# A row softmax with temperature on one core: eight-row tiles under a scheduler against sixteen-row tiles in four-row blocks under a written-out order

## The chip, the cores and the metric

The kernel runs on one core of one Trainium2 chip. The metric is the device time of one execution in microseconds (us), taken as the median of several runs. One further number comes from a profiled execution: its span, from its first to its last instruction, which the views of the profile divide up.

## What is computed

The input has 16 x 1024 rows of 512 float32 values, and each row is put through a softmax after division by 0.5:

```python
x_scaled = x / temp                                   # temp = 0.5
x_max = np.max(x_scaled, axis=-1, keepdims=True)
exp_x = np.exp(x_scaled - x_max)
return exp_x / np.sum(exp_x, axis=-1, keepdims=True)
```

The 16,384 rows come to 33.55 MB, which are read once and written once. A row fits in one partition, so no data passes between partitions.

## The kernel before

The rows are cut into 16 tiles of 128 partitions x G = 8 rows (L26). In the main memory the eight rows of a partition stand one behind the other, so a partition's share of a tile is one run of 16 KB and a tile is 2 MB. The tiles live in a pool of eight buffers (L35), and all work is done in place.

For each tile the loop at L42 issues, in this order:

- the load of the tile on the queue of SyncE (SP), L44;
- one VectorE reduction over all eight rows, giving the negative maximum of each, L47;
- eight ScalarE activations, one a row, exp(2x - max) with the sum of the row as a second output, L51. Subtracting the maximum of x itself, not of 2x, changes numerator and denominator alike;
- the reciprocal of the eight sums on VectorE, L61;
- on VectorE one multiplication of rows 2 to 7 by their reciprocals, the reciprocals being read as a second tensor that is broadcast along the row, L65;
- on ScalarE the scaling of rows 0 and 1, a copy with a per-partition factor, L71;
- the store of the whole tile on the queue of GpSimd (POOL), L78.

Nothing in the kernel fixes how the tiles follow one another on an engine: the tile framework orders the instructions by its own estimate and puts in the waits. A load has to wait for the store of the tile that had its buffer before, eight tiles earlier. The first eight loads wait for nothing.

Of the kernel before, what the change touches and what calls it, by code (L numbers as in the profile page):

```python
# [1 line left out]

# [4 lines left out]


@with_exitstack  # L10
def kernel(
    ctx: ExitStack,
    tc: tile.TileContext,
    x: bass.AP,
    out: bass.AP,
):
    nc = tc.nc
    fp32 = mybir.dt.float32
    P = nc.NUM_PARTITIONS

    D = x.shape[-1]
    xf = x.flatten_outer_dims()
    of = out.flatten_outer_dims()
    N = xf.shape[0]

    G = 8  # L26
    C = N // (P * G)
    assert C * P * G == N

    N_ACT_NORM = 2  # L30

    xr = xf.rearrange("(c p g) d -> c p g d", p=P, g=G)
    outr = of.rearrange("(c p g) d -> c p g d", p=P, g=G)

    data = ctx.enter_context(tc.tile_pool(name="data", bufs=8))  # L35
    stats = ctx.enter_context(tc.tile_pool(name="stats", bufs=8))

    AX = mybir.AxisListType.X
    EXP = mybir.ActivationFunctionType.Exp
    COPY = mybir.ActivationFunctionType.Copy  # L40

    for c in range(C):  # L42
        xt = data.tile([P, G, D], fp32, name="xt")
        nc.sync.dma_start(out=xt, in_=xr[c])  # L44

        negmax = stats.tile([P, G], fp32, name="negmax")
        nc.vector.reduce_max(negmax, xt, axis=AX, negate=True)  # L47

        sums = stats.tile([P, G], fp32, name="sums")
        for g in range(G):  # L50
            nc.scalar.activation(  # L51
                out=xt[:, g, :],
                in_=xt[:, g, :],
                func=EXP,
                bias=negmax[:, g : g + 1],
                scale=2.0,
                accum_out=sums[:, g : g + 1],
            )

        recip = stats.tile([P, G], fp32, name="recip")  # L60
        nc.vector.reciprocal(recip, sums)  # L61

        if N_ACT_NORM < G:
            k = N_ACT_NORM
            nc.vector.tensor_mul(  # L65
                xt[:, k:, :],
                xt[:, k:, :],
                recip[:, k:].unsqueeze(2).broadcast_to((P, G - k, D)),
            )
        for g in range(N_ACT_NORM):  # L70
            nc.scalar.activation(  # L71
                out=xt[:, g, :],
                in_=xt[:, g, :],
                func=COPY,
                scale=recip[:, g : g + 1],
            )

        nc.gpsimd.dma_start(out=outr[c], in_=xt)  # L78


# [1 line left out]
_INS = ['x']  # L82
_OUTS = [((16, 1024, 512), 'float32')]


# [23 lines left out]
```

The softmax here doesn't subtract the row's maximum and nothing guards it: scores larger than these inputs give would overflow.

## Time and profile before

| what | value |
|---|---|
| median of 5 runs | 164.64 us (163.82 to 164.75) |
| the profiled execution's own time | 163.82 us |
| its span | 161.7 us |
| VectorE busy | 124.5 us (77% of the span), 48 instructions |
| ScalarE busy | 112.5 us (70%), 289 instructions |
| GpSimd busy | 8.8 us (5%) |
| moved by DMA | 67.13 MB, mean 415 GB/s over the span |

The profiled execution took 163.82 us, of which 161.7 are its span; the remaining 2.1 us lie around it. It was the quickest of the five runs, 0.82 us under the median, and this distance has to be kept in mind when a sum made on the span is set against the median.

How to read the views: the page begins with busy time by engine; then the span is cut into 40 slices, with a digit for the busy tenth of each engine in a slice, and the mean busy share of the 16 DMA engines below it. After that come the DMA queues (q1 is SyncE's, "hardware_dynamic"; q0 is GpSimd's, "software_dynamic"), the chain of work that ended last, and groups of instructions by line with the mean duration of one in ns. A busy engine is only a bound if the others wait for it in the end.

### The profile page before, as it was taken

Reading aid. Unit: us, or ns where it says so; the run is one execution under the profiler, and the core shown is the slowest. Engines: PE = TensorE matmul, PEld = TensorE weight load, DVE = VectorE, ACT = ScalarE, POOL = GpSimd, SP = SyncE. Lnnn points to the kernel's source line nnn. Section 1 sums busy time; section 2 is a strip of 40 time slices with the busy share of each in tenths; the row PEclk is TensorE's granted clock in tenths of the full one; section 3 lists DMA queues with packets and bytes.
Section 4 is the critical chain, followed back from the end, with each engine's and each line's share of the span. In section 5 each row is a group of like instructions: output and inputs, shape, how many; then the busy total and the mean of one; then the engine's idle time right before and its main releaser. Section 6 shows DMA issues by size and latency. Waiting matters only on the chain.

```text
span 161.7 us, 483 instructions
## 1 busy us (share of the span) xinstructions
DVE 124.5 (77%) x48; ACT 112.5 (70%) x289; POOL 8.8 (5%) x20
## 2 busy tenths in 40 slices
DVE  0088799999999999695986959689595986999100
ACT  0037997999999998949397593957939397595000
POOL 0000010010101010101001010100101001011100
DMA  5999999999999999999999999999999999999993
GB/s 146 438 434 418 446 430 381 422 444 426 426 446 422 426 446 418 434 442 418 438 428 430 434 430 426 442 426 430 438 426 434 438 422 430 442 418 434 413 442 134
DMA packets 4610, 67.13 MB, mean 415 GB/s; under 512 B 512, under 2 KB 512, under 8 KB 512
## 3 DMA queue, kind: packets, MB, share of 16 engines
q1 hardware_dynamic: 2304, 33.56, 49.3%
q0 software_dynamic: 2304, 33.56, 48.6%
q14 instruction: 2, 0.02, 0.0%
HBM read 33.55 MB, written 33.55 MB: 415 GB/s over the span
## 4 chain that ended last, share of the span: by engine, by line
DMA 61%; DVE 18%; ACT 8%; issue 7%; POOLq 0%; SPq 0%
DMA xt<-in_x_dram 37%; DMA out_dram<-xt 23%; DVE negmax L47 11%; ACT xt L51 7%; DVE xt L65 6%; ACT xt L71 1%; DVE recip L61 0%; POOLq L104 0%; SPq L44 0%; POOLq L78 0%
## 5 line engine op out<-in xcount | busy, mean ns | idle before, releaser
L51 ACT ACTIVATE xt<-xt,negmax 128x512 f32<-128x512 f32 x128 | 90.5, 710 | 26.4 <-DVE negmax L47 26.4
L47 DVE TENSOR_REDUCE negmax<-xt 128x8 f32<-128x4096 f32 x16 | 70.4, 4403 | 24.2 <-DMA xt<-in_x_dram 24.2
L65 DVE TENSOR_TENSOR xt<-xt,recip 128x3072 f32<-128x3072 f32 x16 | 53.6, 3350 | 0.1
L51 ACT ACTIVATION_READ_ACCUMULATOR xt<-xt,negmax 128x1 f32 x128 | 24.2, 189 | 0.0
L71 ACT ACTIVATE xt<-xt,recip 128x512 f32<-128x512 f32 x32 | 21.1, 709 | 0.3 <-DVE recip L61 0.3
L78 POOL DMA_DIRECT2D out_dram<-xt x16 | 8.6, 540 | 142.0 <-ACT xt L51 87.4
L51 ACT ACT_TABLE_LOAD x1 | 1.3, 1283 | 8.8 <-DMA xt<-in_x_dram 8.8
L61 DVE RECIPROCAL recip<-sums 128x8 f32<-128x8 f32 x16 | 3.1, 196 | 1.2 <-ACT xt L51 1.2
L93 POOL MEMSET const-float32-0.0<- 128x1 f32 x1 | 0.1, 98 | 0.2 <-issue 0.2
L93 POOL MEMSET const-bfloat16-1.0<- 128x1 bf16 x1 | 0.1, 101 | 0.0
L93 POOL MEMSET const-float32-1.0<- 128x1 f32 x1 | 0.1, 98 | 0.0
L93 POOL MEMSET const-uint8-127<- 128x1 uint8 x1 | 0.1, 98 | 0.0
## 6 DMA issues: line engine op xcount, KB each, us to landing
xt<-in_x_dram SPq DMA_DIRECT2D x16, 2048.0 KB, 26.8
out_dram<-xt POOLq DMA_DIRECT2D x16, 2048.0 KB, 17.9
```

The lines of the kernel that those rows point to most:

```text
L47: nc.vector.reduce_max(negmax, xt, axis=AX, negate=True)
L51: nc.scalar.activation(out=xt[:, g, :], in_=xt[:, g, :], func=EXP, bias=negmax[:, g : g + 1], scale=2.0, accum_out=sums[:, g : g + 1],)
L61: nc.vector.reciprocal(recip, sums)
L65: nc.vector.tensor_mul(xt[:, k:, :], xt[:, k:, :], recip[:, k:].unsqueeze(2).broadcast_to((P, G - k, D)),)
L71: nc.scalar.activation(out=xt[:, g, :], in_=xt[:, g, :], func=COPY, scale=recip[:, g : g + 1],)
L78: nc.gpsimd.dma_start(out=outr[c], in_=xt)
L93: nc = _bacc.Bacc("TRN2", target_bir_lowering=False, num_devices=1)
```

## The change

The tile grows to G = 16 rows (one run of 32 KB a partition, 4 MB a tile, eight tiles), in six buffers. The order on every engine is now the order of the program text (`manual_schedule`). Work goes in blocks of B = 4 rows, 32 in all, and the loop over blocks puts later steps of earlier blocks behind the first steps of the current one: in step i, VectorE gets the maximum of block i and then the scaling of block i - 1; ScalarE gets the exponentials of block i, then the scaling of its one row of block i - 2, then, where block i - 3 was the last of its tile, the store of the whole tile.

The scaling on VectorE becomes three instructions a block, each one row times a per-partition factor. ScalarE scales one row in four, as before. The maximum is multiplied by 2 in a small extra instruction, so 2 max is what is subtracted. Stores leave GpSimd's queue and go to ScalarE's. The first tile is loaded in two pieces: rows 0 to 3 through ScalarE's queue, rows 4 to 15 through SyncE's. A one-element exponential at the start brings the load of the activation table forward.

The core of the diff (function bodies that keep their operation are cut):

```diff
-    G = 8
+    G = 16
+    B = 4
+    N_ACT = 1
-    data = ctx.enter_context(tc.tile_pool(name="data", bufs=8))
-    stats = ctx.enter_context(tc.tile_pool(name="stats", bufs=8))
+    FIRST = [(0, 4), (4, 16)]
+    data = ctx.enter_context(tc.tile_pool(name="data", bufs=6))
+    stats = ctx.enter_context(tc.tile_pool(name="stats", bufs=6))
+    ctx.enter_context(tc.manual_schedule())
-        nc.sync.dma_start(out=xt, in_=xr[c])
+        for lo, hi in FIRST if c == 0 else [(0, G)]:
+            queue = nc.scalar if (c, lo) == (0, 0) else nc.sync
+            queue.dma_start(out=xt[:, lo:hi, :], in_=xr[c][:, lo:hi, :])
-        nc.vector.reduce_max(negmax, xt, axis=AX, negate=True)
+        nc.vector.tensor_reduce(negmax, xb, axis=AX, op=MAX, negate=True)
+        nc.vector.tensor_scalar_mul(bias, negmax, 2.0)
-            nc.vector.tensor_mul(
-                xt[:, k:, :],
-                xt[:, k:, :],
-                recip[:, k:].unsqueeze(2).broadcast_to((P, G - k, D)),
-            )
+        for g in range(B - N_ACT):
+            nc.vector.tensor_scalar_mul(xb[:, g, :], xb[:, g, :], recip[:, g : g + 1])
-        nc.gpsimd.dma_start(out=outr[c], in_=xt)
+    def store(i):
+        c, b = blocks[i]
+        if b + B == G:
+            nc.scalar.dma_start(out=outr[c], in_=tiles[c])
+    load(0)
+    warm = stats.tile([P, 1], fp32, name="warm", bufs=1)
+    nc.vector.memset(warm, 0.0)
+    nc.scalar.activation(out=warm, in_=warm, func=EXP)
+    n = len(blocks)
+    for i in range(n + 3):
+        if i < n:
+            if blocks[i][1] == 0 and i:
+                load(blocks[i][0])
+            shift(i)
+            exponentials(i)
+        if 1 <= i <= n:
+            scale_vector(i - 1)
+        if 2 <= i <= n + 1:
+            scale_scalar(i - 2)
+        if 3 <= i:
+            store(i - 3)
```

`shift` holds the reduction and the doubling, `exponentials` the four exponentials, `scale_vector` the reciprocal and the three products, `scale_scalar` ScalarE's row.

More of the change, by code (lines that the diff above doesn't have):

```diff
@@ L19 @@
     P = nc.NUM_PARTITIONS
+    AX = mybir.AxisListType.X
+    EXP = mybir.ActivationFunctionType.Exp
+    COPY = mybir.ActivationFunctionType.Copy
+    MAX = mybir.AluOpType.max
     D = x.shape[-1]
@@ L24, with load, shift, exponentials @@
     N = xf.shape[0]
-    G = 8
+    G = 16
+    B = 4
+    N_ACT = 1
     C = N // (P * G)
     assert C * P * G == N
-    N_ACT_NORM = 2
     xr = xf.rearrange("(c p g) d -> c p g d", p=P, g=G)
     outr = of.rearrange("(c p g) d -> c p g d", p=P, g=G)
-    data = ctx.enter_context(tc.tile_pool(name="data", bufs=8))
-    stats = ctx.enter_context(tc.tile_pool(name="stats", bufs=8))
[L38 to L43, printed above, removed]
-        nc.sync.dma_start(out=xt, in_=xr[c])
[L46 to L50, printed above, removed]
+    FIRST = [(0, 4), (4, 16)]
+    data = ctx.enter_context(tc.tile_pool(name="data", bufs=6))
+    stats = ctx.enter_context(tc.tile_pool(name="stats", bufs=6))
+    ctx.enter_context(tc.manual_schedule())
+    tiles = {}
+    blocks = [(c, b) for c in range(C) for b in range(0, G, B)]
+    state = {}
+    def load(c):
+        xt = tiles[c] = data.tile([P, G, D], fp32, name="xt")
+        for lo, hi in FIRST if c == 0 else [(0, G)]:
+            queue = nc.scalar if (c, lo) == (0, 0) else nc.sync
+            queue.dma_start(out=xt[:, lo:hi, :], in_=xr[c][:, lo:hi, :])
+    def shift(i):
+        c, b = blocks[i]
+        xb = tiles[c][:, b : b + B, :]
+        negmax = stats.tile([P, B], fp32, name="negmax")
+        nc.vector.tensor_reduce(negmax, xb, axis=AX, op=MAX, negate=True)
+        bias = stats.tile([P, B], fp32, name="bias")
+        nc.vector.tensor_scalar_mul(bias, negmax, 2.0)
+        state[i] = (xb, bias)
+    def exponentials(i):
+        xb, bias = state[i]
+        sums = stats.tile([P, B], fp32, name="sums")
+        for g in range(B):
             nc.scalar.activation(
-                out=xt[:, g, :],
-                in_=xt[:, g, :],
+                out=xb[:, g, :],
+                in_=xb[:, g, :],
                 func=EXP,
-                bias=negmax[:, g : g + 1],
+                bias=bias[:, g : g + 1],
                 scale=2.0,
@@ L58, with scale_vector, scale_scalar @@
             )
-        recip = stats.tile([P, G], fp32, name="recip")
+        state[i] = (xb, sums)
+    def scale_vector(i):
+        xb, sums = state[i]
+        recip = stats.tile([P, B], fp32, name="recip")
         nc.vector.reciprocal(recip, sums)
-        if N_ACT_NORM < G:
-            k = N_ACT_NORM
-            nc.vector.tensor_mul(
-                xt[:, k:, :],
-                xt[:, k:, :],
-                recip[:, k:].unsqueeze(2).broadcast_to((P, G - k, D)),
-            )
[L70 to L75, printed above, removed]
-            )
-        nc.gpsimd.dma_start(out=outr[c], in_=xt)
+        for g in range(B - N_ACT):
+            nc.vector.tensor_scalar_mul(xb[:, g, :], xb[:, g, :], recip[:, g : g + 1])
+        state[i] = (xb, recip)
+    def scale_scalar(i):
+        xb, recip = state[i]
+        for g in range(B - N_ACT, B):
+            nc.scalar.activation(
+                out=xb[:, g, :], in_=xb[:, g, :], func=COPY, scale=recip[:, g : g + 1]
+            )
+    def store(i):
+        c, b = blocks[i]
+        if b + B == G:
[17 more added lines that the diff above has]
+            store(i - 3)
 _INS = ['x']
```

## The prediction

> **What bounds the kernel now.** I read the slices first: does any row stay at 9 from end to end?
>
> ```profile
> DVE  0088799999999999695986959689595986999100
> ACT  0037997999999998949397593957939397595000
> ...
> DMA  5999999999999999999999999999999999999993
> GB/s 146 438 434 418 446 430 381 422 444 426 426 446 422 426 446 418 434 442 418 438 428 430 434 430 426 442 426 430 438 426 434 438 422 430 442 418 434 413 442 134
> ...
> q1 hardware_dynamic: 2304, 33.56, 49.3%
> q0 software_dynamic: 2304, 33.56, 48.6%
> ```
>
> Only the DMA row does; VectorE and ScalarE fall to 3 to 6 in the second half. The two queues carry equal bytes and together fill 97.9% of all 16 DMA engines' time. The chain of waits agrees: most of it is DMA.
>
> ```profile
> DMA 61%; DVE 18%; ACT 8%; issue 7%; POOLq 0%; SPq 0%
> ```
>
> Next the busy time by stretch; the last two columns are the DMA share and GB/s.
>
> ```profile
> 0.00:1.80 1.80, 0.00 (x0) 0.00 (x0) 0.20 (x4) 1.00 0.08 18
> 1.80:4.00 2.20, 0.00 (x0) 0.00 (x0) 0.00 (x0) 1.00 0.90 238
> ...
> 24.00:36.00 12.00, 12.00 (x6) 10.87 (x30) 0.53 (x1) 1.00 1.01 416
> 36.00:134.00 98.00, 83.89 (x33) 78.58 (x205) 5.84 (x11) 1.00 1.01 431
> 134.00:159.00 25.00, 14.72 (x6) 10.91 (x27) 1.59 (x3) 1.00 1.00 427
> 159.00:160.00 1.00, 0.00 (x0) 0.00 (x0) 0.00 (x0) 1.00 0.05 16
> 160.00:161.70 1.70, 0.00 (x0) 0.00 (x0) 0.00 (x0) 1.00 0.00 0
> ```
>
> So the span is this: 1.8 us until data flow; 2.2 us at 238 GB/s, which lose 2.2 x (1 - 238/431) = 1.0; 67.1 MB at 431 GB/s, 155.7; from 159.0 to the end 2.7. That makes 161.2; the other 0.5 are the slower stretches (416 for 12 us loses 0.4, 427 for 25 us loses 0.2). There is no hole in the DMA, so no compute can shorten the middle. What remains open is the ends, the efficiency of a byte, and whether the new order opens a hole.
>
> The queues share evenly. Stores of 2 MB are issued every 9.73 us in the steady part, with a 2 MB load between two of them: 4.19 MB / 9.73 = 431 GB/s.
>
> ```profile
> 84.77 0.53 POOL L78 DMA_DIRECT2D out_dram<-xt  x1 [9.20 <-ACT xt L51]
> 94.50 0.53 POOL L78 DMA_DIRECT2D out_dram<-xt  x1 [9.19 <-ACT xt L51]
> ```
>
> The prices of the compute come from the groups (mean ns of one after the bar):
>
> ```profile
> L51 ACT ACTIVATE xt<-xt,negmax 128x512 f32<-128x512 f32 x128 | 90.5, 710 | 26.4 <-DVE negmax L47 26.4
> L47 DVE TENSOR_REDUCE negmax<-xt 128x8 f32<-128x4096 f32 x16 | 70.4, 4403 | 24.2 <-DMA xt<-in_x_dram 24.2
> L65 DVE TENSOR_TENSOR xt<-xt,recip 128x3072 f32<-128x3072 f32 x16 | 53.6, 3350 | 0.1
> L71 ACT ACTIVATE xt<-xt,recip 128x512 f32<-128x512 f32 x32 | 21.1, 709 | 0.3 <-DVE recip L61 0.3
> L61 DVE RECIPROCAL recip<-sums 128x8 f32<-128x8 f32 x16 | 3.1, 196 | 1.2 <-ACT xt L51 1.2
> ```
>
> [...] (4403 - 3350) / 1024 = 1.03 ns an element, with about 0.16 us fixed. [...] The share of 0.05 between 159 and 160 us is 16 x 0.05 = 0.8 engine-us, which fits one or two late engines.
>
> **The change part by part, against the profiled execution (span 161.7, time 163.82).**
>
> *Bytes and rows.* The bytes stay. A partition's run goes from 16 to 32 KB: 128 fewer rows for each DMA engine (256 to 128). A row now takes, by the queue table, 0.486 x 161.7 x 16 / 2048 = 0.614 us on q0[...]. In the trace's packet records one engine's rows start 0.607 us apart in the last 20 us[...].
>
> *Stores from ScalarE's queue, not GpSimd's.* [...] up to 0.6 at the end goes; I take half, 0.3 (0 to 0.6). Of the 0.4 lost at 416 GB/s, where the first store starts, I take 0.2 (0 to 0.4). The eight DMA issues on ScalarE cost at most 0.53 each (the POOL row), 4 us beside 158 of DMA, with exponentials queued behind them; they are hidden while VectorE is slower than ScalarE (below).
>
> *First piece and warm-up.* The table load (1.28 us) already lay beside the first reduction, so nothing. The first piece has 8 KB rows and competes with 24 KB rows; in turns by packet both end together, 4.19 MB after the start: 1.8 + 1.0 + 9.7 = 12.5 us, against 8.7 for the first tile now. By bytes it would be about 7. Either is off the path: the DMA goes on with the queued loads.
>
> *Compute.* A VectorE block: reduction of 2048 elements, 2048 x 1.03 + 0.16 = 2.27; the doubling, priced like the reciprocal, 0.20; reciprocal 0.20; three products. Product: not in the trace; [...] less up to 0.08 of overlap (the timeline shows a reciprocal starting at 142.50 before the product ended at 142.58), 0.34[...]. I take 0.34. Sum 3.7 us with 0.02 to 0.04 at each handover (bounds 3.5 and 4.5). ScalarE: four exponentials, whose starts in the timeline lie 0.705 apart, 2.8, and one row at 0.6: 3.4. So VectorE sets the pace, 32 x 3.7 = 118 us, under the DMA's 158.
>
> *Does a hole open?* A 4 MB tile takes 9.7 us alone and 19.4 when both queues run. Store 0 sits on ScalarE behind block 6, whose tile must have landed: 12.5 + 2.5 + 7 x 3.7 = 41, moving at 42 (issue to data took 1.1 at the start). By then 39.2 / 9.7 = 4.05 tiles are loaded; the other 3.95 share, so the last load lands at 42 + 3.95 x 19.4 = 118.7, and stores 0 to 3 are nearly done. Store 4 then lasts to 128.9, store 5 to 138.6. Store 6 is the delicate one: its tile's last scaling stands on VectorE behind the reduction of tile 7, and the store behind block 30. From 119: 2.5, twice 3.7, and 3.4 on ScalarE is 13.3: issued at 132.3, moving at 133.4, 5 us before it is needed. By pace alone: 12.5 + 2.5 + 31 x 3.7 = 130. Store 7 comes at about 138, needed at 148. Loads 6 and 7 wait for stores 0 and 1, done at 61 and 81, when loads up to 5 are still running. No hole; the end is data at 2.8 + 16 x 9.7 = 158 and 2.7 after it.
>
> Sum: 0.6 + 0.3 + 0.2 = 1.1 us less: span 160.6, time 162.7 for an execution like the profiled one. The median stood 0.82 above it, so 163.5.
>
> **The rivals.** A change within 0.5% (0.8 us) is about what can't be told from none.
> - *The transfer is what it was*: cost goes by bytes, or a 32 KB run goes out as two packets, and the late engines stay. [...] Time about 164.4.
> - *VectorE becomes the bound (slower)*: [...] The place is store 6, needed at 138.6: (137.5 - 15) / 31 = 3.95 us a block is the point from which it decides, a product step of 0.43 us; beyond it each 0.1 us costs 3 x 31 x 0.1 = 9 us. At 0.61 a block takes 4.5: store 6 at 15 + 31 x 4.5 = 154.5, moving at 155.6, 17 us late, span about 178, time about 180. For it: the trace shows only that rate, and the margin is 0.25 us a block. [...]
> - *The order alone opens a hole*: the first piece lands at 7, store 0 goes out one block earlier and loads share sooner; 3.7 of the 5 us go, and slower handovers take the rest. A hole of 2 to 3 us: about 166.5.
> - *More is gained*: the upper bounds, 1.5 + 0.6 + 0.4 = 2.5: 162.1.
>
> **How the numbers follow.** Likeliest case 0.50 (163.5, own range 162.7 to 164.2); same transfer 0.28; VectorE 0.12; hole from order 0.06; more gain 0.04. Faster by over 0.5% (under 163.8): four fifths of the first case, the last, and a little of the second, 0.46. Slower (over 165.5): VectorE, the hole, and a sliver, 0.19. The rest 0.35. The range 162.6 to 165.8 leaves out the VectorE case, half the hole and the extreme gain.
>
> **What would show it.** In the profile after: DMA at 9 throughout; about 1150 packets in the store queue, not 2304, at over 431 GB/s; product rows at about 420 ns; first maximum near 12.5 us; ScalarE's store 6 issued near 132 while DMA is still full. A product near 690 ns, or a DMA slice under 9 near 140 us, makes the prediction wrong.

## The result and the profile after

The changed kernel takes 163.30 us (median of 29 runs, 162.88 to 166.95), the kernel before 164.29 (50 runs beside them). The ratio of the two is 0.9958, with a 95% interval of 0.9942 to 0.9973: a gain of 0.4%, clear of zero. That is within the 0.5% that was called no change, though the interval reaches to 0.6%. Executions of neither kernel are all alike: those before lie from 163.7 to 165.0, most near 163.8 or near 164.6; of the changed kernel most lie near 163.3 and a fifth near 164.8. The profiled execution took 163.22 us, its span is 161.4, where before it was 163.82 and 161.7.

The slices, queues and chain of the changed kernel (q10 is now ScalarE's queue, which carries the stores and the first 1 MB of the loads):

```profile
DVE  0007899999999999999999999999936999400000
ACT  3001979999999999999999999999980999900000
...
DMA  6999999999999999999999999999999999999992
...
q10 hardware_dynamic: 1296, 34.60, 49.7%
q1 hardware_dynamic: 1152, 32.51, 47.8%
q14 instruction: 4, 0.03, 0.0%
...
DMA 51%; DVE 31%; ACT 4%; issue 1%; SPq 0%
```

The DMA stays at 9 from end to end, as before. VectorE has become nearly as full: it runs at 9 from 20 us to 117. There are 1152 and 1296 packets where there were 2304 a queue: 32 KB of a partition go out as one row, as assumed. The chain names more VectorE and less DMA without the time having risen, so VectorE is taken to be close behind the DMA, not ahead of it; e3 below tests that. One more line deserves attention, that of queue 14: four packets of 8 KB (by the queue's name I take them for fetches of instructions, the engines' own programs), where the kernel before has two.

The groups, with the price that was missing from the trace of before:

```profile
L71 ACT ACTIVATE xt<-xt,bias 128x512 f32<-128x512 f32 x128 | 90.7, 710 | 25.1 <-DVE bias L64 25.1
L62 DVE TENSOR_REDUCE negmax<-xt 128x4 f32<-128x2048 f32 x32 | 73.0, 2280 | 15.9 <-DMA xt<-in_x_dram 15.9
L86 DVE TENSOR_SCALAR xt<-xt,recip 128x512 f32<-128x512 f32 x96 | 40.9, 483 | 1.1
```

A product on VectorE takes 483 ns; in the trace each starts 0.40 us after the one before it, so that three of them fill 1.28 us. A whole block takes 3.79 us, the distance of two reductions there (57.91 and 61.70). The last three lines below are the first reduction of tile 7, the first exponential of block 30, and store 6 going out on ScalarE's queue:

```profile
57.91 2.28 DVE L62 TENSOR_REDUCE negmax<-xt 128x4 f32<-128x2048 f32 x1
60.22 0.17 DVE L64 TENSOR_SCALAR bias<-negmax 128x4 f32<-128x4 f32 x1
60.30 0.17 DVE L84 RECIPROCAL recip<-sums 128x4 f32<-128x4 f32 x1
60.51 1.28 DVE L86 TENSOR_SCALAR xt<-xt,recip 128x512 f32<-128x512 f32 x3
61.70 2.28 DVE L62 TENSOR_REDUCE negmax<-xt 128x4 f32<-128x2048 f32 x1
...
122.36 2.29 DVE L62 TENSOR_REDUCE negmax<-xt 128x4 f32<-128x2048 f32 x1 [3.69 <-DMA xt<-in_x_dram]
...
132.47 0.72 ACT L71 ACTIVATE xt<-xt,bias 128x512 f32<-128x512 f32 x1 [0.25 <-DVE bias L64]
132.50 0.34 ACTq L99 DMA_DIRECT2D out_dram<-xt  x1
```

In the program store 6 stands behind all four exponentials of block 30 and a scaling. It goes out 0.03 us after the first of these exponentials starts, without waiting for the rest; and that first one waited for VectorE's maximum of block 30. VectorE in turn had waited for tile 7 until 122.36.

By the trace's packet records the first data of that store move at 139.1, directly behind those of store 5. It was 5.8 us early (139.1 - 132.5, less 0.8 from issue to data): no hole.

Where did the 0.3 us of span go, then? The packet records give the start and end of every packet, but not the DMA engine that moved it. Each transfer has 16 packets of 4 bytes (272 for the changed kernel's 17); I take the ends of the last store's 16 as the moments at which the 16 engines are done. The span falls into four parts that add up to it. "First data" is the start of the first data packet; "mean finish" is the mean of the 16 moments, counted from the first data; "lag" is how far the last engine comes behind that mean; "end" is from the last engine's finish to the last instruction. The lower rows are the experiments of the next section.

| kernel | first data | mean finish | lag | end | span | fetches |
|---|---|---|---|---|---|---|
| before | 1.78 | 157.48 | 0.65 | 1.78 | 161.7 | 2 |
| changed | 1.72 | 157.09 | 1.29 | 1.27 | 161.4 | 4 |
| changed, once more (e5) | 1.73 | 156.92 | 1.35 | 1.27 | 161.3 | 4 |
| changed, once more (e11) | 1.74 | 157.07 | 1.19 | 1.27 | 161.3 | 4 |
| 16 KB rows (e1) | 1.71 | 157.62 | 1.23 | 1.28 | 161.8 | 5 |
| GpSimd's store queue (e2) | 1.73 | 156.90 | 1.14 | 1.78 | 161.6 | 4 |
| first tile all on SyncE (e4) | 1.72 | 156.89 | 1.78 | 1.28 | 161.7 | 4 |
| idle memsets (e6) | 1.73 | 156.96 | 1.65 | 1.29 | 161.6 | 8 |
| no doubling (e7) | 1.72 | 157.02 | 0.81 | 1.22 | 160.8 | 3 |
| no doubling, one product (e9) | 1.74 | 156.85 | 1.35 | 1.20 | 161.1 | 3 |
| copy, 32 KB, ScalarE (e8) | 1.73 | 156.80 | 0.44 | 1.11 | 160.1 | 0 |
| the same, idle memsets (e12) | 1.73 | 156.90 | 1.90 | 1.23 | 161.7 | 4 |
| copy, 16 KB, GpSimd (e10) | 1.76 | 157.58 | 0.37 | 1.78 | 161.5 | 0 |

From before to changed: mean finish -0.4 (-0.4 to -0.6 over three profiles), end -0.5, lag +0.6. Two gains and one loss that eats about two thirds of them.

The lag is seen in the stretches too. In the changed kernel (DMA share and GB/s last) most engines are done before 159, and what is left runs on one or a few; the kernel before was still at 360 GB/s between 158 and 159:

```profile
134.00:157.00 23.00, 5.00 (x10) 6.78 (x16) 0.00 (x0) 1.00 1.00 433
157.00:158.00 1.00, 0.00 (x0) 0.00 (x0) 0.00 (x0) 1.00 1.06 459
158.00:159.00 1.00, 0.00 (x0) 0.00 (x0) 0.00 (x0) 1.00 0.23 98
159.00:160.00 1.00, 0.00 (x0) 0.00 (x0) 0.00 (x0) 1.00 0.00 0
```

A packet is put down to the moment at which it starts. The last one starts at 158.9 and, being 32 KB long, ends at 160.1.

### The profile page after: what moved, and what is told of

It reads as the page before. It is cut to its first block, busy times and chain, and to the rows that moved or that the text cites. A ratio compares the mean times of both kernels' runs of the same rounds, so it can differ in the third digit from the quotient of the medians.

```text
span 161.4 us, 563 instructions
## 1 busy us (share of the span) xinstructions
DVE 119.5 (74%) x193; ACT 114.7 (71%) x290; POOL 0.2 (0%) x4
## 3 DMA queue, kind: packets, MB, share of 16 engines
q10 hardware_dynamic: 1296, 34.60, 49.7%
q1 hardware_dynamic: 1152, 32.51, 47.8%
## 4 chain that ended last, share of the span: by engine, by line
DMA 51%; DVE 31%; ACT 4%; issue 1%; SPq 0%
DMA xt<-in_x_dram 32%; DVE negmax L62 19%; DMA out_dram<-xt 18%; DVE xt L86 10%; ACT xt L71 3%; DVE bias L64 1%; ACT xt L92 1%; DVE recip L84 1%; SPq L56 0%
## 5 line engine op out<-in xcount | busy, mean ns | idle before, releaser
L71 ACT ACTIVATE xt<-xt,bias 128x512 f32<-128x512 f32 x128 | 90.7, 710 | 25.1 <-DVE bias L64 25.1
L62 DVE TENSOR_REDUCE negmax<-xt 128x4 f32<-128x2048 f32 x32 | 73.0, 2280 | 15.9 <-DMA xt<-in_x_dram 15.9
L86 DVE TENSOR_SCALAR xt<-xt,recip 128x512 f32<-128x512 f32 x96 | 40.9, 483 | 1.1
L71 ACT ACTIVATION_READ_ACCUMULATOR xt<-xt,bias 128x1 f32 x128 | 23.9, 187 | 0.0
L92 ACT ACTIVATE xt<-xt,recip 128x512 f32<-128x512 f32 x32 | 22.4, 706 | 0.0
L84 DVE RECIPROCAL recip<-sums 128x4 f32<-128x4 f32 x32 | 5.5, 171 | 2.2 <-ACT xt L71 2.2
L64 DVE TENSOR_SCALAR bias<-negmax 128x4 f32<-128x4 f32 x32 | 5.4, 170 | 1.1
## 6 DMA issues: line engine op xcount, KB each, us to landing
xt<-in_x_dram SPq DMA_DIRECT2D x1, 3072.0 KB, 12.2
xt<-in_x_dram ACTq DMA_DIRECT2D x1, 1024.0 KB, 12.3
```

The lines of the kernel that those rows point to most:

```text
L62: nc.vector.tensor_reduce(negmax, xb, axis=AX, op=MAX, negate=True)
L64: nc.vector.tensor_scalar_mul(bias, negmax, 2.0)
L71: nc.scalar.activation(out=xb[:, g, :], in_=xb[:, g, :], func=EXP, bias=bias[:, g : g + 1], scale=2.0, accum_out=sums[:, g : g + 1],)
L86: nc.vector.tensor_scalar_mul(xb[:, g, :], xb[:, g, :], recip[:, g : g + 1])
L92: nc.scalar.activation(out=xb[:, g, :], in_=xb[:, g, :], func=COPY, scale=recip[:, g : g + 1])
```

## The experiments

My theory after this reading: the DMA sets the end in both kernels; long rows bring 0.5 us; the queue of the stores brings 0.5 at the end; instruction fetches make the last engine late. The rivals: row length costs nothing; VectorE's pace or the order of the stores decides; the lag is chance. Beside e1 to e4 the nine executions of the kernel before all lay between 164.47 and 164.78, so that the ratios of these four come out about 0.2% lower than that of the changed kernel above. Between experiments the times and the four parts are compared.

**e1, row length alone.**

```diff
-    G = 16
+    G = 8
-    FIRST = [(0, 4), (4, 16)]
+    FIRST = [(0, 4), (4, 8)]
-    data = ctx.enter_context(tc.tile_pool(name="data", bufs=6))
+    data = ctx.enter_context(tc.tile_pool(name="data", bufs=12))
```

> The changed kernel with eight rows a tile (16 KB runs, 2 MB tiles, twelve buffers), all else kept. Theory (the gain is 128 fewer rows for each DMA engine, 0.005 us each, partly eaten by a later last engine): the 16 engines finish 0.6 us later on average, but the last of them lags the mean by some 0.7 us, not 1.4; span 161.0 to 161.7, time 163.2 to 163.7. Rival (row length costs nothing; the gain lies in the queue of the stores): mean finish unchanged, time 162.6 to 162.9, since the lag shrinks. Second rival (shorter tiles end the kernel sooner): under 162.5.

Measured: 163.60 us, ratio to before 0.9932 (0.9920 to 0.9944). The mean finish rises to 157.62, 0.5 to 0.7 above the three profiles of the changed kernel. Over the whole table, the three profiles with 16 KB rows have 157.48 to 157.62 and the ten with 32 KB rows 156.80 to 157.09, whatever else differs. The first rival falls. The lag was expected to shrink to 0.7 and did not, 1.23, with five fetches, so it isn't a matter of one long packet at the end.

**e2, the store queue alone.**

```diff
-            nc.scalar.dma_start(out=outr[c], in_=tiles[c])
+            nc.gpsimd.dma_start(out=outr[c], in_=tiles[c])
```

> The changed kernel with its stores back on GpSimd's queue. Theory (about 0.5 us of the gain is the stretch from the last landing to the end of the span, 1.4 us before and 0.8 after): that stretch goes back to about 1.4 us, time 163.8 to 164.0, DMA finish as in the changed kernel. Rival (the queue of the stores is nothing): 163.3. [...]

Measured: 163.08 us, ratio 0.9900 (0.9885 to 0.9915). The end stretch came back, 1.78 for 1.27, exactly as in the kernel before. Yet the time did not rise to the 163.8 to 164.0 that were expected. Mean finish and lag were a little shorter in its profile (156.90 and 1.14), and its four timed executions, 163.01 to 163.32, lie about the changed kernel's 163.22. So the end stretch belongs to the queue, but that moving the stores brings 0.5 us of time is not shown. No store was held up: GpSimd issued store 0 at 37.83, ScalarE at 37.71.

**e3, VectorE's pace: the rival on the slower side.**

```diff
-        for g in range(B - N_ACT):
-            nc.vector.tensor_scalar_mul(xb[:, g, :], xb[:, g, :], recip[:, g : g + 1])
+        k = B - N_ACT
+        nc.vector.tensor_mul(
+            xb[:, :k, :],
+            xb[:, :k, :],
+            recip[:, :k].unsqueeze(2).broadcast_to((P, k, D)),
+        )
```

> The changed kernel with the three products of a block as one product of two tensors [...] (1536 elements, by the row of the kernel before about 1.73 us against 1.28). A VectorE block takes 3.79 + 0.45 = 4.24 us. Theory (from 3.95 us a block VectorE sets the end): 31 x (4.24 - 3.95) = 9 us late, time 168 to 173, DMA slices under 9 near 140 us. Rival (VectorE's pace is covered, only the order of the last stores counts): 163 to 165.

Measured: 166.33 us, ratio 1.0098 (1.0084 to 1.0111). The mechanism is there, its size is a third of what was expected. The product takes 1758 ns, that is, with L65's 3350 ns for twice the elements, (3350 - 1758) / 1536 = 1.04 ns an element; the rival had taken 1.03 from before (its 690 ns a row are 512 x 1.03 + 160, its step of 0.61 us that less 0.08). The block takes 4.27 us; store 6 goes out at 142.74, and the DMA all but stands still before it:

```profile
L86 DVE TENSOR_TENSOR xt<-xt,recip 128x1536 f32<-128x1536 f32 x32 | 56.3, 1758 | 1.1
```

```profile
140.19 2.28 DVE L62 TENSOR_REDUCE negmax<-xt 128x4 f32<-128x2048 f32 x1
...
142.70 0.72 ACT L71 ACTIVATE xt<-xt,bias 128x512 f32<-128x512 f32 x1 [0.73 <-DVE bias L64]
142.74 0.34 ACTq L103 DMA_DIRECT2D out_dram<-xt  x1
```

```profile
136.00:139.00 3.00, 2.93 (x4) 2.27 (x6) 0.00 (x0) 1.00 1.04 448
139.00:141.00 2.00, 2.00 (x2) 2.00 (x7) 0.00 (x0) 1.00 0.15 66
141.00:142.00 1.00, 1.00 (x1) 0.98 (x3) 0.00 (x0) 1.00 0.00 0
142.00:143.00 1.00, 0.93 (x4) 0.30 (x1) 0.00 (x0) 1.00 0.00 0
143.00:144.00 1.00, 1.00 (x1) 1.00 (x3) 0.00 (x0) 1.00 1.22 524
```

In the first line all is well, in the next three hardly anything new starts (66 GB/s, then none), at 143.6 store 6 begins. (In the same stretches the changed kernel has shares of 0.89, 1.10, 1.21, 0.99 and 0.76.) The size was off because I had let store 6 follow 31 blocks. It follows 30 and the reduction and doubling of the next: the third reduction starts at 20.6, 28 blocks of 4.27 bring the one of block 30 to 140.2, and 2.5 for it and its doubling give 142.7, which is what the trace has. The needed moment, 138.3 at issue, then allows (138.3 - 2.5 - 20.6) / 28 = 4.1 us a block, not 3.95. And with the hole the lag is 0.09, where the changed kernel has 1.29: I take it that the late engine caught up while the others had nothing to move, which no figure here shows.

**e4, the last part of the change undone.**

```diff
-            queue = nc.scalar if (c, lo) == (0, 0) else nc.sync
+            queue = nc.sync
```

> The changed kernel with both pieces of the first tile on SyncE's queue. Theory (the two queues take turns by packet, so the piece on ScalarE's queue lands with the rest; when VectorE starts is off the path): first maximum at about 6.5 us, not 13.1, store 0 some 3.5 us earlier, time unchanged within 0.4 us of 163.3. Rival (an earlier store 0 takes away the cover of store 6, so a hole opens): 164.5 to 166.5, DMA under 9 near 135 us.

Measured: 163.15 us, ratio 0.9912 (0.9898 to 0.9926), the time of the changed kernel. The first reduction starts at 5.44 us; in the changed kernel it starts at 13.09:

```profile
5.44 2.29 DVE L62 TENSOR_REDUCE negmax<-xt 128x4 f32<-128x2048 f32 x1 [4.58 <-DMA xt<-in_x_dram]
```

So putting the first piece on ScalarE's queue didn't make it land early. It made it land with the rest, and the first reduction start 7.6 us later. In the changed kernel's packet records the two queues advance row by row, though the rows of the piece are a third as long: by 9 us 80 of its 128 rows of 8 KB and 96 of the other 128, of 24 KB, have started, by 11 us 112 and 116; the last ones end at 12.5 and 12.2. The time doesn't notice, because when compute starts is off the path. Store 0 went out at 34.2 instead of 37.7, store 6 at 136.4 with data at 138.9: the cover fell from 5.8 to 1.7 us. The rival's mechanism is real, and it stopped 1.7 us short of a hole.

**e5 and e11, the changed kernel again.**

> The changed kernel itself, as the measure for the three others on the same chip. Expected 163.2 to 163.4 us; mean finish of the 16 DMA engines 157 us after the first data, the last engine 1.1 to 1.8 us behind the mean, four instruction fetches of 8 KB within the span.

> The changed kernel again, for a profile of one of its executions near 164.8 us, of which there were some on the two chips before. If the fetches are the cause of those too, two of them fall on one engine late in the run and the last engine is about 3 us behind the mean; if not, the lag is as in the others and the time lies elsewhere: in a hole near 139 us, or in the first 4 us.

Measured: e5 163.70 us (22 runs, ratio 0.9970, 0.9946 to 0.9995), not the 163.2 to 163.4 expected; the profiled execution of e11 took 163.11. Both profiles have nearly the same four parts as the first. But the executions of the changed kernel fall into two groups: of the 49 compared in both sets, 14 took 164.4 to 165.1 us, the others 162.9 to 164.0. No profile fell on one of the upper group, e11 included, so their cause stays open. In e5 they are 8 of 21, which draws its ratio, 0.9970, nearer to 1 than the profiles say.

**e6, more instruction fetches, beside the whole kernel.** The memsets write to a tile of their own.

```diff
+        for _ in range(16):
+            nc.gpsimd.memset(idle, 0.0)
         if 1 <= i <= n:
             scale_vector(i - 1)
```

> The changed kernel with 16 idle one-element memsets on GpSimd in each of the 35 steps, 560 in all; nothing waits for them. Theory (what holds the last DMA engine back is that the instruction fetches, 8 KB at a time, all fall on one engine, each costing it 0.3 us and a slow packet after it): about four more fetches, the last engine 2.5 to 4 us behind the mean, time 164.5 to 166. Rival (the lag is chance at the start of the data): lag 1.1 to 1.8 as before, time 163.2 to 163.5. If the fetches of different engines fall on different DMA engines: more fetches, lag and time little changed.

Measured: 163.66 us, ratio 0.9959 (0.9946 to 0.9973), where the lower group of e5 lies near 163.2 on the same chip. Eight fetches, as expected, and a lag of 1.65, less than expected. Two engines are late here, by 1.6 and 2.2 us against the first to finish. Packets can be followed back from there: wherever only one packet ends near another's start, the overlap of the two is 3 or 4 ns, and I take such a pair to be on one engine. By this link the engine that is last has four fetches on it (at 11.2, 33.6, 57.6 and 83.6). The other four lie near the times of the changed kernel's own (34.1, 47.2, 88.7 and 132.7): those at 46.8 and 134.8 on the engine that is last but one, those at 35.1 and 88.3 elsewhere. So the new fetches made another engine late, not the same one later: the third reading that was written down.

**e7, the doubling left out, which the kernel before does without too.**

```diff
-        bias = stats.tile([P, B], fp32, name="bias")
-        nc.vector.tensor_scalar_mul(bias, negmax, 2.0)
-        state[i] = (xb, bias)
+        state[i] = (xb, negmax)
```

> The changed kernel without the doubling of the maximum, as the kernel before has it: the maximum, not twice the maximum, is subtracted. VectorE loses 32 instructions and about 0.25 us a block. Theory (pace is covered, the DMA sets the end): the time changes only by what the missing instructions spare in fetches, 162.7 to 163.3. Rival (VectorE's pace is what counts): 32 x 0.25 = 8 us, 155.

Measured: 162.74 us, ratio 0.9905 (0.9880 to 0.9930), against 0.9970 for the changed kernel on the same chip: the fastest of the kernels that compute. VectorE's busy time fell by 5 us, to 114.4, its block to 3.60, and the mean finish did not move, 157.02. Pace is covered. What moved is the lag, 1.29 to 0.81, with one fetch less: they stand at 34.0, 51.8 and 85.2, and none near 132.7.

```profile
DVE 114.4 (71%) x161; ACT 114.7 (71%) x290; POOL 0.2 (0%) x4
...
q14 instruction: 3, 0.02, 0.0%
```

**e8, e10, e12: the traffic alone.** The loop holds only a load on SyncE's queue and a store, on ScalarE's for e8 and e12 (32 KB rows, six buffers), on GpSimd's for e10 (16 KB rows, twelve buffers); e12 adds the memsets.

```diff
     for c in range(C):
         xt = data.tile([P, G, D], fp32, name="xt")
         nc.sync.dma_start(out=xt, in_=xr[c])
         nc.scalar.dma_start(out=outr[c], in_=xt)
+    idle = stats.tile([P, 1], fp32, name="idle", bufs=1)
+    for _ in range(560):
+        nc.gpsimd.memset(idle, 0.0)
```

> Loads of 4 MB tiles on SyncE's queue and stores on ScalarE's, six buffers, nothing computed: the input is copied to the output. It is the floor of this traffic. Theory: the same mean finish as in the changed kernel within 0.4 us (its DMA has no hole), no instruction fetches and so a last engine within 0.7 us of the mean: 162.0 to 162.6. Rival (compute still costs the changed kernel something in the middle): under 161.5.

> Loads of 2 MB tiles (16 KB runs) on SyncE's queue and stores on GpSimd's, twelve buffers, nothing computed: the input is copied to the output. It is the floor of the traffic of the kernel before. Theory (the kernel before has no hole either): 0.5 to 0.6 us later mean finish than with 32 KB runs for the rows, 0.6 us more after the last landing for GpSimd's queue: 163.0 to 163.3 us, against 162.0 with 32 KB runs and ScalarE's queue. Rival (the kernel before lost time to its order of work): under 162.5.

> The copy with 32 KB runs (nothing computed, the input is copied) and 560 idle memsets on GpSimd, for which nothing waits. Theory of the fetches: about four fetches within the span, each costing its DMA engine 0.5 to 0.9 us; if all of one instruction stream fall on one engine, the last engine is 2 to 3 us behind the mean and the time 163.5 to 165; if they are spread over engines, 0.7 to 1.2 us and 162.2 to 162.8. Rival (fetches are harmless, compute or its memory traffic makes the last engine late): lag 0.4 as in the copy, 162.0.

Measured: e8 162.01 us, ratio 0.9862 (0.9836 to 0.9889); e10 163.32, 0.9933 (0.9912 to 0.9954); e12 163.78, 0.9970 (0.9958 to 0.9983). So the traffic of the changed kernel has a floor of 162.0 us and that of the kernel before one of 163.3; each kernel lies 1.0 to 1.3 above its own. For the changed kernel 0.85 of that is lag (1.29 and 0.44). The two copies differ by 1.3: 0.8 in the mean finish and 0.7 at the end, less 0.1 of lag. Here, with nothing computed, the gain of the longer rows and of the queue is whole.

e12 decides on the fetches. Its queue 14 and its last stretches, then those of e8:

```profile
q14 instruction: 4, 0.03, 0.0%
```

```profile
157.00:158.00 1.00, 0.00 (x0) 1.00 1.14 492
158.00:159.00 1.00, 0.00 (x0) 1.00 0.08 33
159.00:160.00 1.00, 0.00 (x0) 1.00 0.08 33
```

```profile
157.00:158.00 1.00, 0.00 (x0) 1.00 1.21 524
158.00:159.00 1.00, 0.00 (x0) 1.00 0.01 0
159.00:160.00 1.00, 0.00 (x0) 1.00 0.00 0
```

No engine of compute but GpSimd does anything, and nothing waits for it. Still the time is 1.8 us longer, and a share of 0.08 for two us is one 32 KB packet each: one engine starts another packet when the others are done. It ends 2.2 us after the first to finish, 2.24 / 4 = 0.56 a fetch. The mean finish moved by 0.1 only, so the memsets did not slow the traffic as a whole. In the packet records each fetch takes 0.31 us, and the packet behind it 1.43 to 1.56, not 1.21. By the link of e6 all four fetches lie on the last engine, and they cost it 0.54 + 0.53 + 0.66 + 0.64 = 2.4 us, about what it is late by. In the changed kernel the packet behind a fetch takes 1.46 to 1.75. The fetches at 47.2 and 132.7 lie on its last engine and cost 0.85 + 0.74 = 1.6 us, and it is 1.7 behind the first; the other two lie on the engine that is last but one, 1.1 us of cost and 1.0 behind. That the lag is chance is refuted.

**e9, fewer instructions still:** e7 with the product of e3.

> Without the doubling and with the three products of a block as one product of two tensors: a VectorE block of 4.27 - 0.19 = 4.08 us, 97 instructions on VectorE, not 193. By the corrected count of blocks (store 6 follows 30 of them: 13.1 + 30 x 4.08 + 1.6 = 137.1, its data 0.8 later at 137.9, needed at 139.1) there is no hole, 1.2 us of cover being left. Theory of the fetches: two or three fetches, last engine 0.6 to 0.9 us behind the mean, time 162.4 to 162.8. If the corrected count is wrong as the first was (decision at 3.95): a hole, 164 to 167.

Measured: 163.00 us, ratio 0.9911 (0.9882 to 0.9939). Store 6 goes out at 136.62, expected 137.1 (a count that still gave 1.6 us to the last exponentials), and there is no hole at 4.07 us a block. So the point lies between 4.07 and 4.27, as the corrected count has it. The fetches are three, as in e7, but the lag is 1.35, not 0.6 to 0.9, and the time not the 162.4 to 162.8 expected. By the link of e6 its last engine has at most two of the three, which cost 1.2 us, and it is 1.7 behind the first. The rest is unexplained, so the gain of e7 can't be put down to the number of fetches alone.

## Why the prediction was right where it was right

Predicted 163.5 us, measured 163.3, and the forecast that the DMA sets the end with no hole in it held. That the number is so near is luck. The terms came to 1.1 us less of span and to 162.7 us for an execution like the profiled one; measured were 0.3 us (161.7 to 161.4) and 163.22. The 0.82 us that were then added, because the median stood that far above the profiled execution, made up for it: after the change that distance is 0.08 (163.30 and 163.22), and before the change, by fifty executions instead of five, it was 0.47. Step by step:

- *Rows:* 0.6 us saved was an estimate of mine: the trace of before has rows of 16 KB starting 0.607 us apart on one engine, but nothing that shows what a longer row costs. Now rows of 32 KB start 1.209 apart, not 2 x 0.607 = 1.214, and 0.005 x 128 is 0.6. Between e1 and the changed kernel the mean finish differs by 0.5 to 0.7. Right.
- *Late engines:* -0.3 was taken, +0.6 came. This step failed, with the wrong sign. That GpSimd's queue makes engines late was a guess, which no trace of before shows. The changed kernel does not use that queue and has the longer lag, 1.29 for 0.65; with GpSimd's queue put back (e2) the lag is 1.14, in the copy with that queue (e10) it is 0.37. The line of queue 14 stood on the page of before with two packets, and I read past it. What the runs show in its place: two of the changed kernel's four fetches lie on its last engine and cost it 1.6 us. The change raises VectorE's instructions from 48 to 193; that the two new fetches are of VectorE's program is likely, but the trace doesn't say whose they are.
- *The end:* left at 2.7 us. From the last engine's finish it is 1.78 with GpSimd's queue (before, e2, e10) and 1.1 to 1.3 with ScalarE's. That -0.5 was missing from the sum. With -0.4 for the mean finish, +0.6 for the lag and -0.5 for the end, the 0.3 us of span are accounted for.
- *First store's dip:* -0.2 was taken. It is contained in the mean finish and can't be told apart in it.
- *Block:* 3.7 predicted, 3.79 measured. The product's row is 483 ns, not 420, its step 0.40, not 0.34 (both were estimates, since before no product of this form was in the trace); between the reduction and the first product 0.32 pass for the doubling and the reciprocal, not 0.40. The fixed part of an instruction was also misread: with 1.03 ns an element, 3350 ns for 3072 elements leave 0.19 us, not 0.16. That three products by a per-partition factor take less than one product of two tensors was right: e3 shows the other, 1.76 us for three rows against 1.28.
- *Point of decision:* 3.95 us a block was mis-sized by one block; measured between 4.07 (e9) and 4.27 (e3). By the wrong point the true block had 0.16 us left, by the right one about 0.3. The same slip put store 0 at 41, and it was at 37.7.
- *Store 6:* 132.3 predicted, 132.5 measured, by two errors that cancel. Tile 7 was to be there at 119 and VectorE got it at 122.36. The 3.4 us of ScalarE's work put between VectorE and the store were not there.
- *First piece and warm-up:* 12.5 predicted by turns, 13.1 measured; off the path, as e4 shows. The table load starts at 1.16 us, where it started at 8.77; neither held up the first exponential, which in both kernels started behind the first maximum, at 13.17 before and at 15.62 now.
- *Own range and chances:* the gain is 0.4% by the ratio, which is the case "within 0.5%", given 0.35, not the likeliest, 0.46; the medians, 164.29 and 163.30, are 0.6% apart, so it is close to the line. Of the likeliest case the rows and the missing hole were right, the late engines and the end were not.

Open: why executions differ by 0.8 us before and 1.5 after, why e2 is not slower though its end is, and the rest of the lag of e9.

## What to carry to other kernels

When the DMA is full from end to end, price its parts by the finish of each engine: the mean tells what the traffic costs, the last one what the kernel waits for (from e8 to e12 the mean moved by 0.1 us, the last by 1.6 and the time by 1.8). Here instructions cost time even on an engine for which nothing waited: 560 memsets brought the copy four fetches and those 1.8 us; leaving out the doubling brought about 0.5 us against the lower group on its chip (e7), an earlier start of compute nothing (e4). And for the cover of a late store, count the blocks ahead of it one by one, and see in the trace which of them it waits for.

## What the runs showed of the hardware that I had not expected

- An instruction fetch of 8 KB took 0.31 us, and the 32 KB packet behind it on the same engine, by the link of e6, 1.43 to 1.75 for 1.21 (changed kernel and e12). With four of them, all on one engine, the copy took 1.8 us more (162.01 to 163.78).
- Two queues of unequal rows shared by rows, not by bytes: a piece of 1 MB in 8 KB rows beside one of 3 MB in 24 KB rows landed 12.3 us after its issue, the 3 MB 12.2 after theirs. Queued ahead of the rest on one queue (e4), the 1 MB was there 4.7 us after its issue.
- With the stores on GpSimd's queue the kernel ended 1.78 us after the last DMA engine was done (before, e2, e10), on ScalarE's 1.1 to 1.3.
- A store that the program puts on ScalarE behind four exponentials and a scaling went out as soon as the first of these exponentials had started, not after the last: 37.71 after 37.68 for store 0, 132.50 after 132.47 for store 6.
